# Neighbourhood attention on 4-row by 32-column key blocks, with values beside ones and the gated convolution run between the heads

## The chip, the cores and the metric

The kernel runs on the 8 cores of one Trainium2 chip, each core with its own part of the batch. The metric is the device time of the slowest core in microseconds (us). Most executions agree within 0.3%. Some fall in a slow state, in which the cores of one die get a lower clock; only fast executions are compared here (die 0 is cores 0 to 3, die 1 cores 4 to 7), and stage lengths are medians over the eight cores of the profiled execution.

Names: PE is TensorE (matmuls), ACT is ScalarE, DVE is VectorE, POOL is GpSimd, SP is SyncE, whose queue issues part of the DMAs; "POOLq" and "SPq" are the queues' issues. L0 to L3 are the four layers; 0 and 2 are "even", 1 and 3 "odd". The even part of a layer is everything from its first projection to the end of its out-projection; its MLP follows. "Modulation tiles" are pieces of ada_w, the weights that give shift, scale and gate; a tile is 1024 x 512 weights.

## The reference, cut to what matters

```python
# four layers; two request groups share the weights: 512 prompt tokens and 1024 latent tokens
# (a grid of 16 rows x 64 columns) per core
for l in range(4):
    # c: one vector for the latent tokens, another for the prompts; ada_w[l]: 1024 x 6144
    sh1, sc1, g1, sh2, sc2, g2 = ada_mod(silu(c), ada_w[l], ada_b[l])
    h = rms_norm(y, norm1_g[l]) * (1 + sc1) + sh1
    if l % 2 == 0:
        bg, cg, xa, q, k, v = split(h @ w_in, 6)        # 512 columns each
        a = bg * short_conv(cg * xa, conv_w)            # the gated conv, width 3 over tokens
        q, k = rms_norm(q, gq), rms_norm(k, gk)         # per head, 8 heads of 64
        # prompt: dense attention.  latent: each query sees 8 rows x 16 columns of keys
        # around it (clamped at the edges), with a relative bias, plus 256 cached keys,
        # all in one softmax
        mix = concat([a, att]) @ w_out
    else: ...                                            # pooling and latent attention, not touched
    y = y + g1 * mix
    y = y + g2 * sq_relu_mlp(rms_norm(y, norm2_g[l]) * (1 + sc2) + sh2, w1[l], w2[l])
```

## The kernel before

A program builder records operations with what they read and write, and a list scheduler fixes, before the run, the order of each engine by a "key" (lower goes first among what is ready in its model). Every engine then runs its own list strictly in order. The parts that the change and the argument touch:

```python
NW = 2                                  # two weight buffers of 1024 x 512 bf16, used in turn
def wtile(srcs, key=None):
    s = wt_i[0] % NW; wt_i[0] += 1      # strict turn: tile n waits until tile n-2 is used up
    DMA("pool", [(WT[s][...], src) ...], [], [bWT[s]], "wt%d" % s)

def norm(l, which, tb, key=None):       # 512 tokens, 8 slices of 128 features
    # ... sum of squares, rstd ...
    for kc in range(8):
        STT(tm, yT[:, kc], A, rstd, mult, mult)              # DVE, fp32
        ACT(hT[:, kc], tm, AF.Identity, bias=shift)          # ACT, to bf16

def even_layer(l, extra_steps):         # extra_steps: layer 0's own eight ada_w tiles
    for j in range(4):                  # gated conv, all of it ahead of the attention
        w = wtile(...)                  # ... 9 groups of 8 matmuls, DVE and ACT work
    for which in (q, k):                # q, then k: project, square, sum by matmul, scale
        # ... and for k a second projection in token order, for the output
    for tt in range(12): ...            # values, token order
    for ex in extra_steps: ex()
    # attention, one latent head: 2 query halves x (6 key tiles of 2 rows x 64 columns + 2 cached)
    for tile in tiles:                  # scores of 512 queries
        MMG(scores); ACT(P, scores, Exp); TT(P, P, table, mult)      # table = exp(bias) x mask
    for tile in tiles:
        MMG(po, V_tile, P)              # values
        MMG(pd, ones, P)                # the softmax sum, as a matmul of its own
    out_proj(...)

def mlp(l, with_ada):
    # 16 weight tiles through wtile; the next layer's 12 ada_w tiles through two buffers
    # of their own in the arena (AW), one step after each half of the work
```

Of the kernel before, what the change touches and what calls it, by code (L numbers as in the profile page):

```python
# [18 lines left out]
class Buf:  # L19

    __slots__ = ("name", "lw", "rd", "excl", "tile")

    def __init__(self, name, excl=False, tile=None):
        self.name = name
        self.lw = []
        self.rd = []
        self.excl = excl
        self.tile = tile


class PV:
# [9 lines left out]
    def rearrange(self, s, **kw):  # L41
        return PV(self.tile, self.chain + ((1, s, kw),))
# [47 lines left out]
class Prog:  # L90
# [18 lines left out]

    def region(self, lo, hi, n=1, name="r"):  # L110

        prior, keep = set(), []
        for (a, b, bl) in self.regions:
            if a < hi and lo < b:
                for x in bl:
                    prior.update(x.lw)
                    prior.update(x.rd)
                if not (lo <= a and b <= hi):
                    keep.append((a, b, bl))
            else:  # L120
                keep.append((a, b, bl))
        out = self.bufs(n, name)
        for x in out:
            x.lw = sorted(prior)
        keep.append((lo, hi, out))
        self.regions = keep
        return out

    def add(self, engs, fns, reads, writes, dur, kind="op", key=None, sem=None, nbytes=0):
# [6 lines left out]
        deps = set()  # L136
        for b in reads:
# [180 lines left out]
    def emit(self):  # L318
# [10 lines left out]
        for nd in self.seq:  # L329
            e = nd.eng  # L330
            kn = know[e]
            need = {}
            for d in sorted(nd.deps, key=lambda d: -nodes[d].fin):
# [50 lines left out]
def _const_tables():  # L384
    kc = np.arange(64)[:, None]
    qc = np.arange(64)[None, :]
    qcs = np.clip(qc - 8, 0, 48)
    colvalid = ((kc >= qcs) & (kc < qcs + 16)).astype(np.float32)
    MF = np.zeros((128, 14, 64), np.float32)
    MI = np.zeros((128, 14, 64), np.float32)  # L390
    for a in range(2):
        for ei in range(14):
            e = 6 - ei
            if -7 <= e + a <= 7:
                MF[a * 64:(a + 1) * 64, ei, :] = colvalid
            if -4 <= e + a <= 3:
                MI[a * 64:(a + 1) * 64, ei, :] = colvalid
# [22 lines left out]
    return dict(MF=MF.reshape(128, 896), MI=MI.reshape(128, 896), PA=PA.reshape(128, 2560), CS=CS,  # L420
# [3 lines left out]
def _rpb_expand(rpb):  # L424
    a = np.arange(128)[:, None, None] // 64
    kc = np.arange(128)[:, None, None] % 64
    e = 6 - np.arange(14)[None, :, None]
    qc = np.arange(64)[None, None, :]
    dr = np.clip(e + a + 7, 0, 14) + 0 * qc
    dc = np.clip(kc - qc + 15, 0, 30) + 0 * e  # L430
    out = rpb[:, :, dr, dc]
    return np.ascontiguousarray(out.transpose(0, 2, 1, 3, 4)).reshape(2, 128, 8 * 896)


def build(depth=4):
# [26 lines left out]
    gktok = din("gktok", (128, 128))  # L462
    rpbx = din("rpbx", (2, 128, 8 * 896))
    MFd = din("MF", (128, 896))
    MId = din("MI", (128, 896))
# [24 lines left out]
    with ExitStack() as st:  # L490
# [24 lines left out]
        gktok_sb = sb("gktok_sb", (128, 2, 64))  # L515
# [12 lines left out]
        rstd = [sb("rstd%d" % i, (128, 512)) for i in range(2)]  # L528
# [137 lines left out]

        def DMA(q, pairs, reads, writes, sem, out=False, key=None):
# [23 lines left out]
        def wtile(srcs, key=None):  # L691
            s = wt_i[0] % NW
            wt_i[0] += 1
            DMA("pool", [(WT[s][:, 0:src.shape[1], c0:c0 + nc_], src) for (c0, nc_, src) in srcs], [], [bWT[s]],
# [8 lines left out]
        def rstd_from(ss, bss, npart, ncol, inv_n, key=None):  # L703
            i = rs_i[0] % len(rstd)
            rs_i[0] += 1
            r, br = rstd[i], brstd[i]
# [10 lines left out]
               (gktok_sb[:], gktok.rearrange("p (i d) -> p i d", i=2)),  # L717
# [63 lines left out]
        def norm(l, which, tb, key=None):  # L781
# [11 lines left out]
            for kc in range(8):  # L793
# [3 lines left out]
                ACT(hT[:, kc, blk(tb)], tm[:], AF.Identity, [btm, bmw], [bh[tb][kc]],  # L797
                    bias=mod[:, l, sh0 + kc, m:m + 1], key=key)
# [383 lines left out]
        def even_layer(l, extra_steps):  # L1182
# [11 lines left out]
            V, bV = ar.take((128, 14, 512), BF16, 14, "V")  # L1194
            sqr = Ring([ar.take((128, 512), BF16, 1, "sq") for _ in range(2)])
            MFs, bM = ar.take((128, 896), BF16, 1, "MF")
            MIs, bM2 = ar.take((128, 896), BF16, 1, "MI")
            ost = Ring([ar.take((128, 512), F32, 1, "ost")])
            u0 = ar.off
            cgb, bcg = ar.take((128, T), F32, 1, "cg")  # L1200
            ub, bub = ar.take((128, T), F32, 1, "ub")
# [3 lines left out]
            segs = [(0, 256), (256, 512), (512, 1536)]  # L1205
            for j in range(4):
                w, bw = wtile([(0, 128, W[:, :, j * 128:(j + 1) * 128]),
                               (128, 128, W[:, :, 512 + j * 128:512 + (j + 1) * 128]),
                               (256, 128, W[:, :, 1024 + j * 128:1024 + (j + 1) * 128])])
                pr = lambda tb, o: [(w[:, kc, o:o + 128], hT[:, kc, blk(tb)]) for kc in range(8)]  # L1210
                for tb in range(3):
                    pt = PT(P)
                    MMK(pt[:], pr(tb, 128), [bw] + bh[tb], [pt.b])
                    COPY(cgb[:, blk(tb)], pt[:], [pt.b], [bcg], eng="act")
                for tb in range(3):
                    pt = PT(P)
                    MMK(pt[:], pr(tb, 256), [bw] + bh[tb], [pt.b])
                    TT(ub[:, blk(tb)], pt[:], cgb[:, blk(tb)], ALU.mult, [pt.b, bcg], [bub])
                ACT(cgb[:], ub[:], AF.Identity, [bub, bsm], [bcg], scale=cw[:, i, 1, j:j + 1])
                for (s0, s1) in segs:  # L1220
                    STT(cgb[:, s0 + 1:s1], ub[:, s0:s1 - 1], cw[:, i, 0, j:j + 1], cgb[:, s0 + 1:s1],
                        ALU.mult, ALU.add, [bub, bcg, bsm], [bcg])
                    STT(cgb[:, s0:s1 - 1], ub[:, s0 + 1:s1], cw[:, i, 2, j:j + 1], cgb[:, s0:s1 - 1],
                        ALU.mult, ALU.add, [bub, bcg, bsm], [bcg])
                for tb in range(3):
                    pt = PT(P)
                    MMK(pt[:], pr(tb, 0), [bw] + bh[tb], [pt.b])
                    TT(aT[:, j, blk(tb)], pt[:], cgb[:, blk(tb)], ALU.mult, [pt.b, bcg], [baT[tb][j]])
            LOADC([(kcT[:], nakT[i].rearrange("p (c t) -> p c t", c=4))], [bkc], q="pool")
            LOADC([(V[:, 12:14, :], nav[i].rearrange("(c p) n -> p c n", p=128))], bV[12:14], q="pool")  # L1230
            LOADC([(MFs[:], MFd)], [bM], q="pool")
            LOADC([(MIs[:], MId)], [bM2], q="pool")
            P.key = K + 2
            qv = qTm.rearrange("p (j two) t -> p j two t", two=2)
            for tb_ in range(3):
                MEMSET(qv[64:128, :, 0, blk(tb_)], 0.0, bq[tb_])
                MEMSET(qv[0:64, :, 1, blk(tb_)], 0.0, bq[tb_])
            for which, gain in ((3, gqna_sb), (4, gkna_sb)):
                w, bw = wtile([(0, 512, W[:, :, which * 512:(which + 1) * 512])])
                for j in range(4):  # L1240
                    for tb in range(3):
                        pt = PT(P)
                        MMK(pt[:], [(w[:, kc, j * 128:(j + 1) * 128], hT[:, kc, blk(tb)]) for kc in range(8)], [bw] + bh[tb], [pt.b])
                        sq, bsq = sqr.next()
                        ACT(sq[:], pt[:], AF.Square, [pt.b], [bsq])
                        p2 = PT(P)
                        MMK(p2[:], [(bdiag[:], sq[:])], [bsq, bconst], [p2.b])
                        r, br = rstd_from(p2[:], p2.b, 128, 512, 1.0 / 64)
                        if which == 3:
                            for a in range(2):  # L1250
                                ps_ = slice(a * 64, a * 64 + 64)
                                STT(qTm[ps_, 2 * j + a, blk(tb)], pt[ps_, :], gain[ps_, i:i + 1], r[ps_, :], ALU.mult, ALU.mult,
                                    [pt.b, br, bsm], [bq[tb][2 * j + a]])
                        else:
                            STT(kT[:, j, blk(tb)], pt[:], gain[:, i:i + 1], r, ALU.mult, ALU.mult, [pt.b, br, bsm], [bk[tb][j]])
                if which == 4:
                    for tt in range(4):
                        pt = PT(P)
                        MMK(pt[:], [(hT[:, kc, tt * 128:(tt + 1) * 128], w[:, kc, :]) for kc in range(8)], [bw] + bh[0], [pt.b])
                        o, bo = ost.next()  # L1260
                        ACT(o[:], pt[:], AF.Square, [pt.b], [bo])
# [26 lines left out]
            for ex in extra_steps:  # L1288
                P.key = K + 31
                ex()  # L1290
# [173 lines left out]
```

## Time and profile before

| | before |
|---|---|
| median of fast runs | 2731.5 us (2730.2 to 2736.1) |
| even part of layer 0, of layer 2 | 348.5, 332.1 us |
| the four MLPs | 351.6, 352.7, 351.0, 335.8 us |
| the two odd parts | 283.1, 279.9 us |
| start, up to the first projection | 82.4 us |

A stage is read like this (stretches of the kernel before, the even parts of layers 0 and 2 on its slowest core; columns: start:end, length, then busy us and count of PE, PE weight loads, DVE, ACT, POOL, then the granted clock as a share of full speed, the DMA engines' share (packet times over the engines' time, so it can exceed 1), GB/s):

```profile
83.90:435.30 351.40, 304.27 (x1558) 138.28 (x1587) 182.29 (x387) 207.95 (x369) 33.38 (x41) 0.95 0.45 70
1425.50:1758.20 332.70, 288.59 (x1310) 127.84 (x1334) 178.03 (x378) 205.10 (x364) 38.65 (x41) 0.98 0.32 51
```

PE is busy for 87% of both. The layers run the same code, but layer 0 also loads and uses eight modulation tiles; it is 16 us longer, and its DMA share is 0.45 instead of 0.32.

### The profile page before, as it was taken

The page shows a single profiled execution, that of the slowest core. Times are in us where ns is not written, and L with a number is a line of the kernel's source. Part 1 is how long each engine was busy: PE and PEld are TensorE (multiplying, and loading weights), DVE is VectorE, ACT ScalarE, POOL GpSimd, SP SyncE. Part 2 cuts the span into 40 slices and gives each one's busy share as a digit, 9 for nine tenths or more (in the row PEclk, how much of TensorE's full clock was granted, in tenths as well). Part 3 has the DMA queues.
Part 4 walks back from the last instruction along what each step waited for, and adds up shares of the span by engine and source line. Part 5 has one row for each costly group of instructions (what it writes and reads, how often), then busy time and mean ns, then how long its engine had stood idle before and what let it go on. Part 6 is the DMA issues. An engine that isn't in the chain of part 4 may idle for free.

```text
span 2729.1 us, 39242 instructions; the slowest of 8 cores (2711.3 to 2729.1 us)
## 1 busy us (share of the span) xinstructions
PE 2425.8 (89%) x14026; PEld 1153.1 (42%) x14266; DVE 1222.4 (45%) x2028; ACT 1171.4 (43%) x1866; POOL 246.0 (9%) x315
## 2 busy tenths in 40 slices
PE   1689799999986788999998888999999869899999
PEld 0234334444443454444433333444444435444444
DVE  0553555444455315443454547544345623354443
ACT  2347765112266596122142688512214748632111
POOL 2100010000003100000011100100100120000000
PEclk9899999999999899999999999999999979999999
DMA  9434936346412206456543222554552120133334
GB/s 181 49 45 77 148 54 99 62 78 103 67 30 33 39 2 94 68 80 104 86 61 39 51 50 36 88 80 78 94 88 41 33 46 1 16 47 62 47 47 124
DMA packets 190413, 179.39 MB, mean 66 GB/s; under 512 B 42320, under 2 KB 178512, under 8 KB 190224
## 3 DMA queue, kind: packets, MB, share of 16 engines
q0 software_dynamic: 174032, 149.34, 37.0%
q1 hardware_dynamic: 16192, 27.53, 3.3%
q8 instruction: 119, 1.95, 0.3%
q14 instruction: 70, 0.57, 0.1%
HBM read 312.90 MB, written 11.67 MB: 119 GB/s over the span
## 4 chain that ended last, share of the span: by engine, by line
PE 75%; ACT 7%; DMA 7%; issue 4%; DVE 4%; SPq 2%; POOL 1%; DVEq 0%; ACTq 0%; POOLq 0%
PE psall L595 75%; ACT arena L619 5%; DMA WT<-even_w_in 2%; DMA WT<-ada_w 2%; SPq L668 2%; DMA WT<-mlp_w 1%; DVE arena L630 1%; ACT rstd L619 1%; DMA arena<-ada_w 1%; ACT hT L619 1%; DVE ntmp L641 1%; POOL rtmp L630 1%; PE psall L603 1%; DVE arena L641 0%; POOL arena L630 0%
## 5 line engine op out<-in xcount | busy, mean ns | idle before, releaser
L595 PE MATMUL psall<-hT,WT 128*128 128x512 bf16 x4734 | 1084.4, 384 | 37.9 <-ACT hT L619 22.7
L619 ACT ACTIVATE arena<-psall 128x512 bf16<-128x512 f32 (+4 forms) x919 | 535.3, 611 | 1132.7 <-PE psall L595 1050.6
L595 PEld LDWEIGHTS psall<-hT,WT 128*128 128x128 bf16 x4848 | 475.2, 99 | 609.3 <-issue 66.9
L595 PE MATMUL psall<-arena,WT 128*128 128x512 bf16 x3199 | 714.2, 380 | 7.1 <-DMA WT<-mlp_w 3.2
L641 DVE SCALAR_TENSOR_TENSOR yT<-psall,mod,yT 128x512 f32<-128x512 f32 x480 | 360.1, 751 | 464.3 <-PE psall L595 464.1
L595 PEld LDWEIGHTS psall<-arena,WT 128*128 128x128 bf16 x3264 | 318.4, 98 | 387.7 <-issue 7.2
L595 PE MATMUL psall<-arena 128*128 128x65 bf16 (+6 forms) x2914 | 394.6, 267 | 67.5 <-ACT arena L619 36.0
L641 DVE SCALAR_TENSOR_TENSOR arena<-psall,arena 128x512 bf16<-128x512 f32 x384 | 264.2, 691 | 385.1 <-ACT arena L619 385.1
L595 PEld LDWEIGHTS psall<-arena 128*128 128x128 bf16 (+1 forms) x2936 | 186.6, 98 | 226.0 <-issue 121.9
L619 ACT ACTIVATE arena<-psall,rk 128x1024 bf16<-128x1024 f32 (+1 forms) x224 | 189.4, 951 | 14.7 <-PE psall L595 14.1
L668 POOL DMA_DIRECT2D WT<-mlp_w x64 | 56.0, 875 | 1311.9 <-PE psall L595 1291.6
L619 ACT ACTIVATE nsq<-yT 128x1024 bf16<-128x1024 f32 x96 | 99.6, 1053 | 137.3 <-PE psall L595 107.8
L641 DVE SCALAR_TENSOR_TENSOR ntmp<-yT,A,rstd 128x512 f32<-128x512 f32 x192 | 135.8, 747 | 37.5 <-ACT rstd L619 20.5
L619 ACT ACTIVATE hT<-ntmp,mod 128x512 bf16<-128x512 f32 x192 | 131.4, 717 | 44.0 <-DVE ntmp L641 43.3
L630 DVE TENSOR_TENSOR arena<-arena 128x256 bf16<-128x256 bf16 (+1 forms) x352 | 116.2, 356 | 42.0 <-ACT arena L619 23.0
L595 PE MATMUL psall<-WT,hT 128*128 128x512 bf16 (+1 forms) x631 | 113.0, 331 | 22.5 <-ACT hT L619 7.8
L595 PE MATMUL psall<-arena,ones 128*128 128x512 bf16 (+1 forms) x348 | 118.5, 370 | 10.1 <-ACT arena L619 4.6
L619 ACT ACTIVATE rstd<-rstd 128x512 f32<-128x512 f32 (+2 forms) x148 | 85.7, 580 | 7.1 <-ACT rstd L619 0.7
L595 PEld LDWEIGHTS psall<-WT,hT 128*128 128x128 bf16 x640 | 50.7, 101 | 81.3 <-issue 32.9
L603 PE MATMUL psall<-ident,arena 128*128 128x128 bf16 (+1 forms) x316 | 29.2, 245 | 51.9 <-POOL arena L630 44.8
L595 PE MATMUL psall<-sTb,WT 128*128 128x2 bf16 x384 | 11.6, 164 | 66.0 <-DVE gqr_sb L635 49.8
L619 ACT ACTIVATE rstd<-psall,eps_sb 128x512 f32<-128x512 f32 x84 | 57.4, 683 | 28.4 <-PE psall L595 27.8
(86 smaller groups left out, 912.7 us busy)
## 6 DMA issues: line engine op xcount, KB each, us to landing
WT<-mlp_w POOLq DMA_DIRECT2D x64, 1024.0 KB, 8.3
arena<-ada_w POOLq DMA_DIRECT2D x36, 1024.0 KB, 12.6
WT<-ada_w POOLq DMA_DIRECT2D x12, 1024.0 KB, 12.4
arena<-rpbx SPq DMA_DIRECT2D x16, 448.0 KB, 3.7
yT<-xT SPq DMA_DIRECT2D x3, 2048.0 KB, 25.6
WT<-even_w_in POOLq DMA_DIRECT2D x24, 256.0 KB, 5.9
WT<-even_w_in POOLq DMA_DIRECT2D x6, 1024.0 KB, 9.1
yT_out<-yT SPq DMA_DIRECT2D x6, 1024.0 KB, 4.1
```

Of the source, the lines that this page charges most:

```text
L595: h.matmul(R(out), lhsT=lhsT, rhs=rhs, start=start, stop=stop, skip_group_check=skip))
L603: fns = [lambda h, o=o, a=a: h.transpose(R(o), a, ident[:, :]) for (o, a) in items]
L619: return lambda h: h.activation(out=R(out), in_=R(in_), func=func, **kw)
L630: P.add(eng, [lambda h: h.tensor_tensor(out=R(out), in0=R(in0), in1=R(in1), op=op)], reads, writes, vdur(fsize(out), eng, isb(out, in0, in ...
L641: P.add("dve", [lambda h: h.scalar_tensor_tensor(out=R(out), in0=R(in0), scalar=scalar, in1=R(in1), op0=op0, op1=op1)], reads, writes, vdu ...
L668: fns = [lambda h, o=o, i_=i_: h.dma_start(out=o, in_=i_) for (o, i_) in pairs]
```

## The change

The intent is to take PE work off the even layers. Keys are stored in blocks of 4 rows x 32 columns; for each block the only queries that can see it are 40 columns wide, so scores and values are computed on strips of 8 or 12 rows x 40 columns. Values stand beside 64 columns of ones, so that one matmul gives the output and the softmax sum. The conv, which needs PE much and ACT little, is placed between the heads, which are the other way round. Queries and values are now projected first, keys after them; a second projection of the prompts' keys, only for the output, is gone. Some of the norms' shift-adds (and multiplications of the conv) may run on POOL, and a POOL instruction now waits for the one before it.

```diff
+        def SHIFT(out, in_, v, op, reads, writes, key=None):
+            P.add(("act", "dve", "pool"), {"act": [fa], "dve": [fv], "pool": [fv]}, reads, writes,
+                  {"act": act_dur(out, v, None), "dve": ..., "pool": vdur(n, "pool") + 0.1}, key=key)   # model: 0.685 us
@@ norm
-                ACT(hT[:, kc, blk(tb)], tm[:], AF.Identity, [btm, bmw], [bh[tb][kc]], ...)
+                SHIFT(hT[:, kc, blk(tb)], tm[:], mod[...], ALU.add, [btm, bmw], [bh[tb][kc]], key=key)
@@ even_layer
-            V, bV = ar.take((128, 14, 512), BF16, 14, "V")
+            Vx, bv_ = ar.take((128, 14, 4, 192), BF16, 29, "V")     # value | ones | value per head pair
+            MEMSET(Vx[:, :, :, 64:128], 1.0, [bones])
+            def v_tile(vt):
+                # ... prompt tiles straight; latent tiles by way of a buffer (two in turn):
+                v_, bv = vtr.next()
+                EVAC(v_[:], pt[:], [pt.b], [bv])
+                # 2 column blocks x 2 rows x 2 heads = 8 small DMAs put 32 tokens each in their block
+                DMA("sp", prs, [bv], [...], "vx%d" % (vt % 4))
+            conv_zone = [6, 7]                     # two PSUM banks kept for the conv
+            P.key = K + 15                         # after the heads' keys (K + 10 to K + 12): a filler
+            for j in range(4):
+                w, bw = wtile(...)                 # the conv's tile
+                # ...
+                for ex in extra_steps[2 * j:2 * j + 2]:
+                    ex()                           # layer 0: two modulation tiles after each
+            RG = [(0, 8, 0, 4), (0, 12, 0, 0), (4, 16, 1, 0), (8, 16, 1, 0)]     # query rows per key block
+                        MMG([(scores strip of 40 columns) for b in range(2)], ...)
+                        ACT(pv, sv, AF.Exp); TT(pv, pv, tv, ALU.mult)
+                        # values and sum in one: stationary = vo(...) = 64 values beside 64 ones
 # cuts marked by "..." and by comments
```

## The prediction

> **What bounds the kernel now.** I read the page first (busy shares, the 40 slices, the chain that ended last), then the groups by shape, then the chain in order of time inside the two even layers, then a table of stretches.
>
> ```profile
> PE 2425.8 (89%) x14026; PEld 1153.1 (42%) x14266; DVE 1222.4 (45%) x2028; ACT 1171.4 (43%) x1866; POOL 246.0 (9%) x315
> PE   1689799999986788999998888999999869899999
> ACT  2347765112266596122142688512214748632111
> DMA  9434936346412206456543222554552120133334
> PE 75%; ACT 7%; DMA 7%; issue 4%; DVE 4%; SPq 2%; POOL 1%; DVEq 0%; ACTq 0%; POOLq 0%
> ```
>
> TensorE (PE) is busy in nearly every slice, and three quarters of the chain are its matmuls. So what a change takes off PE counts almost in full, so long as nothing else becomes the wait there. One slice is 68 us: the first even layer is slices 1 to 5, the second 20 to 25.
>
> The price of a matmul comes from the chain inside the even layers:
>
> ```profile
> 223.03 10.74 PE psall L595 x49
> 233.82 10.74 PE psall L595 x49
> 1556.52 10.74 PE psall L595 x49
> ```
>
> 49 matmuls of 512 columns in 10.74 us are 0.219 us each. (The group's mean of 384 ns is latency, as matmuls are pipelined.) I price PE by columns: 0.219 us per 512.
>
> Where the even layers idle shows in the stretches (start:end, length, then busy us and count of PE, PEld, DVE, ACT, POOL, then clock, DMA share, GB/s):
>
> ```profile
> 200.00:256.00 56.00, 53.06 (x239) 24.26 (x245) 19.32 (x27) 35.64 (x66) 6.14 (x6) 0.97 0.30 60
> 256.00:300.00 44.00, 31.13 (x320) 17.80 (x322) 19.93 (x57) 32.60 (x72) 4.71 (x6) 0.91 0.95 146
> 300.00:340.00 40.00, 34.63 (x209) 15.77 (x211) 26.59 (x82) 30.62 (x58) 2.62 (x3) 0.93 0.81 139
> 1487.00:1550.00 63.00, 52.83 (x237) 22.95 (x241) 34.47 (x48) 35.05 (x60) 5.17 (x5) 1.00 0.35 59
> 1590.00:1640.00 50.00, 37.83 (x192) 16.76 (x193) 29.06 (x84) 44.62 (x93) 0.70 (x1) 1.00 0.21 40
> 1640.00:1706.00 66.00, 55.52 (x243) 23.75 (x246) 45.90 (x144) 56.05 (x108) 3.48 (x4) 1.00 0.22 37
> ```
>
> The attention (256 to 383 and 1590 to 1706) keeps ScalarE (ACT) up to 89% busy, and PE waits there for exponentials. In layer 0 the DMA engines are at 0.95 as well: eight modulation weight tiles (ada_w) go through the two weight buffers. So the even layers are PE-bound, with ACT and, in layer 0, DMA close behind.
>
> **What the Trainium skill says.** "TensorE: Matmul & The Clock Gate", section "Wait — 56ns, not 53.3ns?": a warm matmul takes N / 2.4 GHz plus about 2.5 ns, 215.7 ns at 512 columns. The trace agrees (219). So strips of 160 to 480 columns should cost by their columns.
> "ScalarE: Activation LUTs", section "What ACT_TABLE_LOAD costs": an ACTIVATE takes 186 ns + 0.833 ns per column, and back-to-back ones overlap by about 93 ns. The trace agrees: 599 ns for 512 columns, 1053 for 1024, and seven of 512 in a row in 3.54 us, 0.51 each. Fewer, wider exponentials are cheaper.
> "VectorE: DVE Perf Modes", section "Mode 2×_1P — pack two bf16 into one 32-bit read": packed bf16 operands give two results per cycle. The mask multiplies fit it (256 columns in 283 ns, against 684 for 512 from PSUM).
> "DMA: Bandwidth & Descriptors", section "Specifications": transfers under 512 B fall below line rate and turn into read-modify-write. No run here isolates it yet; the new copies of V are made of 128 B pieces.
>
> **The change part by part**, for one even layer (there are two).
>
> 1. **Attention on PE.** Before, a latent head does 2 query halves x 8 key tiles x 3 matmuls (scores, values, ones) x 512 columns = 24,576 columns. After, scores take 3,200 columns (strips of 8, 12, 12, 8 rows x 40 columns x 2 column blocks), values 3,200, the context keys 2 x 2,048: 10,496. The ones come free, as the stationary tile now holds values beside ones. Eight heads save 112,640 columns. The prompt heads go from 3,072 to 2,048 each: 8,192 saved. The second key projection (token order, only for the output) goes: 32 matmuls, 16,384 columns. Sum 137,216 columns = 268 x 0.219 = 58.7 us. The order of instructions of both kernels confirms the sum over two layers (704 matmuls gone, 320 strips new). **Two layers: 117.5 us of PE work.**
>
> 2. **ACT in attention.** By 0.07 us + 0.833 ns per column (the pitch fitted to 0.50 at 512): a latent head has two exponentials of 1,024, two of 960, two of 640, four tables of 480, and Ln and Exp of 1,024 for the denominator: about 8.5 us, 68 for eight heads, against 77 + 20 + 8 = 105 before (128 x 0.60, 16 x 1.2, 8 x 0.95). Per head PE has 10,496 columns = 4.5 us. Alone the heads would thus be ACT-bound; this is why the gated convolution (36 groups of 8 matmuls, 63 us) is run between them.
>
> 3. **The convolution as filler.** In layer 2 the order puts about 9 groups beside the key projection, 11 beside the prompt heads and the rest, then 8 out-projection groups, into the first six latent heads. Heads: PE 36 + 28 + 14 = 78 us against ACT 68 + 6; about 86 us with latencies. The last two heads have no filler: about 8 us lost.
>
> 4. **Weights.** The key weights reuse the query's buffer and are loaded only after the last query matmul. Such a load took 9.1 us; nearly nothing covers it: 6 to 9 us idle per layer. Before, three such loads stood in the chain but cost PE only 1.5 + 2.0 + 2.1 us.
>
> 5. **Copies of V.** 64 small DMAs per layer, 8 for each of 8 latent V tiles, 128 pieces of 128 B each. Old small DMAs took 0.33 to 0.59 us to issue; at 0.4, a tile needs 3.2 us on the queue, against 3.7 us of PE work between V tiles (17 matmuls). By packets: hardware packets cost 3.3% x 16 x 2729 / 16,192 = 89 ns; 1,024 x 89 / 16 = 5.7 us per tile. It may just keep up, or hold the evacuations back; I put 5 us per layer.
>
> 6. **DVE and POOL.** Mask work falls from 160 x 0.28 + 32 x 0.27 + 16 x 1.09 = 71 us to about 16 x 0.48 + 16 x 0.65 = 18 per layer; DVE was not the bound. 52 of 192 shift-adds of the norms move to POOL, where a 512-column cast took 0.61 us: no worse than ACT's 0.72. No gain, perhaps 4 us of loss.
>
> **Sum.** Second even layer now: 1425 to 1706, 281 us, holding 1064 + 64 matmul equivalents (247 us) and 2 of norm: 32 idle. After: 58.7 less work; idle 4 (start) + 7 (keys) + 5 (V) + 12 (heads) + 6 (end) = 34. First: 84 to 383, 299 us: 247 + 10 (ada and norm) and 42 idle; after, 45, since about 30 MB (eight ada tiles and a weight tile of 2 MB, three conv tiles of 1.5, tables of 7.8) must come in some 100 us, and two ada tiles in flight took 12.6 us, 320 MB/ms. Net 117.5 - 2 - 3 - 4 = 108 us: 2731 - 108 = **2623 us**.
>
> **Rivals.**
> (a) **ACT takes over the heads**: a single accumulator and in-order exponentials make each head take ACT's 8.5 us plus 3 to 4 us of waits for the denominator. For it: the 89% of the stretch 1590 to 1640. Against: the filler has its own two banks. 8 heads x 2 layers x 2 us = 32 us back: 2655.
> (b) **V copies and table loads hold the queue**: tiles at 6 us instead of 3.7 make 18 us per layer, and a late table blocks ACT in order; tables are 32 per layer instead of 8. For it: the 89 ns per packet. Against: tables landed in 3.7 us. 2640 to 2670.
> (c) **Layer 0 becomes DMA-bound** at 0.95 share: 20 to 30 us of its gain lost, 2650.
> (d) **Better than summed**: queries and values of the first token block come first, so the norm of the other blocks is hidden (before, PE waited 9.1 us there): 2605.
>
> **Range and chances.** PE's 117 us is near certain. (a) to (c) could each take 20 to 35 and are partly exclusive; (d) gives 10 to 20. I take 2623, 2580 to 2672. Faster by over 2% means below 2677: 0.88; within 2%: 0.10; slower: 0.02.
>
> **What will show it.** PE matmul columns down by 137,216 per layer, and strips priced by columns; spans of both even layers about 56 us shorter, MLP and odd layers equal; heads with PE over 80% busy; one idle of 6 to 9 us for the key weights; V tiles at 4 us with little wait for arena copies. Wrong if: strips run slower than by columns, evacuations wait for the copies by over 10 us per layer, ACT over 95% with PE under 75% in the heads, or norms lengthened by POOL elsewhere.

## The result

| | before | after |
|---|---|---|
| median of fast runs | 2731.5 us | 2673.0 us (2668.9 to 2675.0) |
| ratio of fast runs | | 0.978 (95%: 0.976 to 0.980) |
| even part of layer 0 | 348.5 | 334.4 |
| even part of layer 2 | 332.1 | 280.3 |
| the four MLPs | 351.6, 352.7, 351.0, 335.8 | 352.6, 354.5, 354.2, 342.4 |
| the two odd parts | 283.1, 279.9 | 279.2, 283.2 |
| start | 82.4 | 76.5 |

A ratio is the mean time of one kernel's fast runs over that of the other's in the same rounds, so it isn't quite the ratio of the medians; stage lengths are from the profiled run. The kernel is faster by 2.2%. The predicted 2623 was 50 us too low, and the result lies 1 us beyond the upper end of the range.

The page of the kernel after (busy shares, the 40 slices, and the chain that ended last by engine):

```profile
PE 2343.6 (88%) x13818; PEld 1117.1 (42%) x13818; DVE 1125.4 (42%) x1644; ACT 1079.8 (40%) x1586; POOL 375.1 (14%) x407
PE   1777768999987788999997798999998779899999
ACT  2566514111266595121145576411126659522111
DMA  9356794346312205556533546555631220233334
PE 72%; DMA 6%; ACT 6%; issue 4%; POOL 4%; DVE 4%; SPq 3%; DVEq 0%; POOLq 0%; ACTq 0%
```

PE is busy for 82 us less than before, but slices 1 to 5, the even part of layer 0, show only sevens and a six, and slice 5 has DMA at 9. POOL is now 4% of the chain and was 1%.

The stretches of the kernel after (columns as above): the even parts of layers 0 and 2, and one pause inside layer 0.

```profile
78.00:418.80 340.80, 254.06 (x1489) 120.15 (x1488) 139.45 (x204) 171.72 (x244) 61.67 (x74) 0.88 0.61 99
1405.20:1686.50 281.30, 237.43 (x1108) 108.88 (x1109) 130.03 (x186) 172.02 (x246) 62.16 (x67) 0.93 0.48 82
333.00:361.00 28.00, 2.46 (x75) 2.13 (x74) 1.02 (x2) 0.00 (x0) 5.93 (x10) 0.56 1.20 158
```

Both layers lost about 50 us of PE busy time. In layer 2 that is the gain, 52 us. In layer 0 only 14 us of it came out, and between 333 and 361 us PE stands almost still while the DMA engines are full. The clock column has fallen too, from 0.98 to 0.93 in layer 2.

What holds PE in that pause (the chain in order of time: start, us, what):

```profile
283.45 12.75 DMA WT<-even_w_in
...
333.80 26.84 DMA WT<-ada_w
```

The second line is the last of layer 0's own modulation tiles. In PE's fixed order it stands behind the first two modulation steps of the *next* layer, and all their loads are in flight at once.

The second surprise is POOL. The groups by shape: output<-input, count, busy us and mean ns of one, idle time before it and what ended it; then the chain at the norm that follows layer 3's odd part:

```profile
L622 ACT ACTIVATE hT<-ntmp,mod 128x512 bf16<-128x512 f32 x132 | 92.0, 721 | 81.7 <-DVE ntmp L644 81.6
L672 POOL TENSOR_SCALAR hT<-ntmp,mod 128x512 bf16<-128x512 f32 x52 | 100.1, 1924 | 131.7 <-DVE ntmp L644 123.9 <-POOL hT L672 6.0 <-DVE mod L633 1.0
```

```profile
2326.76 2.07 POOL hT L672
...
2329.04 2.07 POOL hT L672
...
2331.32 2.07 POOL hT L672
```

The same shift-add takes 0.72 us on ACT and 1.92 us on POOL. Five of them stand one after another there, 2.28 us apart (three are shown); PE runs out of other work during the third and waits 4.9 us for hT.

The third is the issue of the value copies (SP's queue: count, then minimum, median and maximum ns of one issue):

```profile
L679 SPq DMA_DIRECT2D arena<-arena x142: 562/601/1886, 90.6 to 2158.1; - x142
L679 SPq DMA_DIRECT2D arena<-rpbx x64: 327/328/952, 185.8 to 1630.1; - x64
```

A plain table load takes 0.33 us to issue, a copy from SBUF to SBUF 0.60. Eight of them with their gaps make 5.1 us per value tile, while PE needs 3.7 us for the work between two tiles.

So there were four suspects: the order of layer 0's loads, POOL, the value copies, and whatever lowers the clock.

### The profile page after: what moved, and what is told of

The parts are those of the page before. It is cut to its first block, busy times and chain, and to the rows that moved or that the text cites. A ratio compares the mean times of both kernels' runs of the same rounds, so it can differ in the third digit from the quotient of the medians.

```text
span 2670.9 us, 37465 instructions; the slowest of 8 cores (2654.4 to 2670.9 us)
## 1 busy us (share of the span) xinstructions
PE 2343.6 (88%) x13818; PEld 1117.1 (42%) x13818; DVE 1125.4 (42%) x1644; ACT 1079.8 (40%) x1586; POOL 375.1 (14%) x407
## 4 chain that ended last, share of the span: by engine, by line
PE 72%; DMA 6%; ACT 6%; issue 4%; POOL 4%; DVE 4%; SPq 3%; DVEq 0%; POOLq 0%; ACTq 0%
PE psall L598 72%; ACT arena L622 4%; SPq L679 3%; POOL hT L672 2%; DMA WT<-ada_w 2%; DMA WT<-even_w_in 1%; DMA WT<-mlp_w 1%; DVE arena L633 1%; DVE ntmp L644 1%; ACT rstd L622 1%; PE psall L606 1%; POOL rtmp L633 1%; ACT hT L622 0%; DVE arena L644 0%; POOL arena L633 0%
## 5 line engine op out<-in xcount | busy, mean ns | idle before, releaser
L598 PE MATMUL psall<-hT,WT 128*128 128x512 bf16 x4656 | 1065.5, 387 | 58.1 <-POOL hT L672 23.0
L622 ACT ACTIVATE arena<-psall 128x512 f32<-128x512 f32 (+6 forms) x721 | 470.8, 662 | 1114.0 <-PE psall L598 1055.2
L598 PE MATMUL psall<-arena,WT 128*128 128x512 bf16 x3456 | 759.5, 381 | 3.6 <-DMA WT<-mlp_w 2.0
L598 PEld LDWEIGHTS psall<-hT,WT 128*128 128x128 bf16 x4656 | 458.3, 99 | 618.3 <-issue 108.9
L598 PEld LDWEIGHTS psall<-arena,WT 128*128 128x128 bf16 x3456 | 337.8, 98 | 412.5 <-issue 12.5
L598 PE MATMUL psall<-arena 128*128 128x65 bf16 (+9 forms) x2872 | 324.9, 261 | 53.9 <-ACT arena L622 23.8
L622 ACT ACTIVATE hT<-ntmp,mod 128x512 bf16<-128x512 f32 x132 | 92.0, 721 | 81.7 <-DVE ntmp L644 81.6
L672 POOL TENSOR_SCALAR hT<-ntmp,mod 128x512 bf16<-128x512 f32 x52 | 100.1, 1924 | 131.7 <-DVE ntmp L644 123.9
L598 PE MATMUL psall<-WT,hT 128*128 128x512 bf16 (+1 forms) x576 | 99.8, 329 | 12.2 <-ACT hT L622 7.2
L598 PE MATMUL psall<-nsq,ones 128*128 128x512 bf16 x192 | 57.8, 418 | 16.5 <-ACT nsq L622 16.5
## 6 DMA issues: line engine op xcount, KB each, us to landing
WT<-ada_w POOLq DMA_DIRECT2D x12, 1024.0 KB, 13.3
```

Of the source, the lines that this page charges most:

```text
L598: h.matmul(R(out), lhsT=lhsT, rhs=rhs, start=start, stop=stop, skip_group_check=skip))
L622: return lambda h: h.activation(out=R(out), in_=R(in_), func=func, **kw)
L672: fv = lambda h: h.tensor_scalar(out=out, in0=in_, scalar1=v, scalar2=None, op0=op)
```

## The experiments

Each was run beside the kernel before on the same chip; the kernel before had 2732.9 to 2734.4 us there, so totals of two runs can differ by some 3 us for the chip alone. Totals are medians of fast runs (e4, e5, e6, e9, e10, e11 and e12 had one slow execution each, left out); stage lengths are from the profiled run.

| run | total | even L0 | even L2 | four MLPs | ratio to before |
|---|---|---|---|---|---|
| kernel after | 2673.0 | 334.4 | 280.3 | 352.6, 354.5, 354.2, 342.4 | 0.978 |
| e1, no shift-add on POOL | 2640.7 | 328.0 | 277.5 | 347.4, 348.1, 348.1, 336.0 | 0.967 |
| e2, next layer's loads held | 2654.0 | 315.6 | 281.3 | 355.1, 354.6, 354.5, 342.2 | 0.972 |
| e4, seven of layer 0's loads left out | 2635.5, disturbed | 290.2 | 280.6 | 354.3, 355.0, 354.8, 342.6 | 0.967 |
| e5, values without copies | 2679.3, disturbed | 323.1 | 272.7 | 366.8, 354.4, 355.1, 342.3 | 0.981 |
| e6, conv ahead of the heads | 2676.7 | 315.2 | 300.4 | 355.4, 355.5, 354.4, 341.9 | 0.979 |
| e7, three mends | 2627.5 | 316.1 | 270.2 | 348.3, 348.3, 348.2, 336.3 | 0.961 |
| e8, PE kept busy in one pause | 2671.7 | 332.5 | 279.9 | 352.5, 354.8, 353.6, 342.3 | 0.977 |
| e9, e7 and two tiles later | 2609.7 | 302.8 | 271.2 | 349.5, 348.7, 348.0, 336.7 | 0.955 |
| e12, ada tiles first, nothing else | 2647.6 | 304.4 | 281.7 | 357.3, 355.8, 354.2, 342.1 | 0.969 |
| e10, e9 with L0's conv ahead | 2620.9 | 317.9 | 268.4 | 348.9, 348.8, 348.0, 335.9 | 0.959 |
| e11, e9 with ada tiles first | 2596.8 | 286.5 | 270.1 | 349.7, 349.0, 348.0, 336.4 | 0.950 |

### e1: no shift-add on POOL

```diff
-            P.add(("act", "dve", "pool"), {"act": [fa], "dve": [fv], "pool": [fv]}, ...
+            P.add(("act", "dve"), {"act": [fa], "dve": [fv]}, ...
```

> Edit: the shift-adds of the norms and of the gated conv may go to ACT or DVE only, never to POOL. Theory P (a POOL shift-add takes 1.92 us against about 0.7 on ACT, and runs of five to twelve of them stand in the chain at the ends of the norms): the PE pauses behind hT from POOL, 4 to 6 us at four norm ends and some smaller ones, go; total 12 to 25 us less, about 2655, with the MLP stages 2 to 5 us shorter each. Rival (POOL was a real relief): ACT gets 52 x 0.7 = 37 us more work and the time stays within 5 us or grows.

Measured: 2640.7 us, 32 less than the kernel after. Every MLP stage, which holds the ends of the norms, is 5.2 to 6.4 us shorter; layer 0 is 6.4 and layer 2 is 2.8 us shorter. The groups of e1 show who took the 52 over:

```profile
L622 ACT ACTIVATE hT<-ntmp,mod 128x512 bf16<-128x512 f32 x174 | 119.5, 717 | 36.3 <-DVE ntmp L644 35.9 <-issue 0.2
L672 DVE TENSOR_SCALAR hT<-ntmp,mod 128x512 bf16<-128x512 f32 x18 | 8.6, 484 | 0.9
```

ACT took 42 of them and DVE 10, at 0.72 and 0.48 us each, and ACT's idle time before them fell from 81.7 to 36.3 us. The theory held, and its size was too small: the gain exceeds the 12 to 25 us expected. The scheduler had POOL at 0.685 us in its model and handed it work it took 1.92 us for. In the trace the duration does not follow what DVE does at the same time: an instruction with 19% of its time beside a busy DVE took 1.76 us and one with 84% took 1.55 us, so sharing with DVE does not explain it. Why this instruction is slow on POOL stays open. (The edit also takes four of the conv's multiplications off POOL, 2.0 and 3.0 us each; they are part of the 32 us.)

### e2: the next layer's loads held back

```diff
-                        DMA("pool", [(w[:], src)], [], [bw], s)
+                        DMA("pool", [(w[:], src)], [bmodB[l - 1]], [bw], s)   # after the layer's own modulation
```

> Edit: the loads of the next layer's modulation weights wait until the previous layer's modulation is finished, so in layer 0 they no longer go ahead of the last own modulation tile and the out-projection. Theory L1 (order of loads): the 26 us that PE stands between 333 and 361 us shrink to 10 or less, and the even part of layer 0 goes from 334 to about 318; all other stages unchanged; total about 2657. Rival L2 (the two weight buffers and the DMA engines' rate limit the layer, whatever the order): less than 6 us, and the pause only moves.

Measured: 2654.0, 19 less; the even part of layer 0 went from 334.4 to 315.6, against the 318 expected, and its MLP is 2.5 us longer, since the loads come later. The order of loads is a cause. It isn't all of it: 315.6 is still 34 us more than layer 2 of the same run.

### e4: layer 0's own modulation loads left out (wrong result)

```diff
+                    if slots is None and nt > 4:
+                        w, bw = hT[:, :, 0:512], bh[0][0]      # no load: any data already there
-                    if slots is None:
+                    elif slots is None:
```

> Wrong result on purpose. Edit: seven of the eight modulation tiles of layer 0 in the even part are computed from activations already in SBUF, so their 15 MB are never loaded; the matmuls stay. Theory L (the loads through two weight buffers took layer 0's gain): the even part of layer 0 falls from 334 to 280 to 292 us, the length that the same code has in layer 2 (280); total 2620 to 2630. Rival (layer 0 is long for another reason, as its cold start or the shift-adds): it stays above 310.

Measured: with seven of the eight loads left out, the even part of layer 0 is 290.2 us, inside the range expected, and 44 us less than with them. So that is what these seven loads, and the work that waits behind them, cost the kernel after. The total must not be read: in two of the four runs a pair of cores (4 and 5, then 2 and 3) was 31 to 64 us slower than the same cores in the profiled run, at a lower clock. The profiled run, in which no pair was hit, took 2631.1, 1 us above the expected range.

### e5: values written straight to their place (wrong result)

```diff
-                v_, bv = vtr.next()
-                EVAC(v_[:], pt[:], [pt.b], [bv])
-                # ... 8 small DMAs
+                EVAC(vpair(vt), pt[:].rearrange("p (j s e) -> p j s e", j=4, s=2), [pt.b], bV[vt])   # token order
```

> Wrong result on purpose. Edit: the latent value tiles are written from PSUM straight to their place, in token order, so the 64 small copies per even layer go away. Theory V (a copy takes 0.60 us to issue, eight of them 5.1 us per tile against 3.7 us of PE work, so the queue paces the value tiles): the query and value phase of both even layers shortens by 5 to 10 us each, and the half-rate matmuls that follow its pauses go too; total 10 to 20 us less. Rival (PE waits there for the norm and for weights anyway): under 4 us in total.

Measured: layer 0 is 11.3 us and layer 2 7.6 us shorter, 19 together: the upper end of what was expected. The total of 2679.3 says the opposite. The mean clock and span of the two dies in the profiled run:

```profile
die 0 (median of its cores): 2668.3 us, clock 0.943
die 1 (median of its cores): 2644.2 us, clock 0.956
```

On die 0 one stage alone, the MLP of layer 0, took 380 us on all four cores and 353 on die 1. The trace says why: for some 155 us of it the granted clock of these four cores is 0.81, and a matmul of 512 columns comes every 260 ns instead of every 216. In the other fast runs the spans of one pair of cores, or of three, are longer at a lower clock. On the undisturbed die the kernel takes 2634 to 2651 us, against 2654 to 2671 on the eight cores of the kernel after. The mechanism is shown by the stages; the total is left out. (Values in a wrong order passed the comparison with the reference. Its tolerance doesn't see them; this kernel is wrong all the same.)

### e6: the conv ahead of the heads again

```diff
-            conv_zone = [6, 7]
-            P.key = K + 15
+            conv_zone = None
+            P.key = K + 5
```

> Edit: one part of the change undone. The gated conv gets back its place ahead of the heads and all PSUM banks; the new key blocks, values beside ones and shift-adds stay. Theory F (alone, a latent head is paced by ACT at 8.5 us plus a wait for its denominator, against 4.5 us of PE work, so the conv between the heads is worth what PE would idle): heads at 9 to 11 us each, and the even part of layer 2 goes from 280 to 310 to 325 us; layer 0 by less, 10 to 30, as its loads are the limit; total 2715 to 2740, so most of the whole gain is lost. Rival (the removed PE columns are the gain, and the conv's place is worth little): less than 10 us per layer.

Measured: 2676.7 (2673.6 to 2682.5), no clear difference from the kernel after. Neither theory had it: layer 2 is 20 us *longer*, less than expected, and layer 0 is 19 us *shorter*. The stretches of e6, even parts of layers 0 and 2:

```profile
77.00:401.00 324.00, 257.11 (x1338) 118.60 (x1360) 133.57 (x196) 179.18 (x256) 50.42 (x66) 0.89 0.59 95
1394.50:1696.80 302.30, 246.90 (x1087) 111.32 (x1109) 129.08 (x184) 175.32 (x250) 55.97 (x65) 0.90 0.44 77
```

The ends of the heads tell why. In layer 2 the eight latent heads end 10.7 us apart with the conv ahead and 11.9 us apart with the conv between them. So a head alone takes 10.7 us, not much more than ACT's work for it (61.9 us in the time of seven heads on the slowest core, 8.8 each, where the prediction had 8.5), and 1.2 us more with its share of the conv and of the out-projection; the filler is worth 20 us in layer 2, where it is fed. In layer 0 the last head of the kernel after ends at 251 us of the stage, but the stage goes on to 334, 83 us; in layer 2 that tail is 34 us. With the conv ahead the tail of layer 0 is 34 us as well. So the 49 us more of tail seem to be work that had been waiting for loads while the heads ran. This is a new theory, which e12 tests: between the heads, a conv tile keeps its weight buffer as long as the heads take (four tiles over some seven heads of 11.9 us, so an estimate of 20 us), and the modulation tiles queue behind it. (A third weight buffer would test that directly. It needs 8 KB per partition and was not run; no run shows whether it fits.)

### e8: PE kept busy in one pause

```diff
+            if l == 2:
+                pw_ = PT(P)        # 36 matmuls that nothing reads, in the pause
+                MMG([(pw_[:], hT[:, kc % 8, 0:128], hT[:, kc % 8, blk(0)], kc == 0, kc == 35) for kc in range(36)],
+                    bh[0] + [bq[2][5]], [pw_.b], key=K + 1.95)
```

> Edit: in layer 2 only, 36 matmuls that nothing reads stand where PE pauses for the key weights (1465.7 to 1474.3 us, two pauses of 4.8 and 3.6 us, after which 12 matmuls came at 427 ns instead of 216). Theory W (after a pause PE runs at half rate for some microseconds, so a pause costs more than its length): the key projections then start at 216 ns each, and the even part of layer 2 gets 2 to 3 us shorter though PE does 7.8 us more work; number of slow matmuls in that stage down by about 12. Rival (the slow matmuls come from elsewhere, as shared power or SBUF traffic of the incoming weights): they stay at 427 ns, and the stage is as long or longer.

The stretches of the kernel after, then of e8, both on core 6: the pause or what fills it, and the 10.8 us that follow in two halves.

```profile
1465.70:1474.30 8.60, 0.77 (x2) 0.13 (x2) 1.73 (x3) 2.40 (x4) 2.58 (x3) 0.73 1.40 154
1474.30:1479.70 5.40, 5.40 (x13) 1.92 (x14) 0.01 (x1) 0.60 (x1) 0.00 (x0) 0.50 1.03 152
1479.70:1485.10 5.40, 5.40 (x26) 2.44 (x25) 1.67 (x3) 1.32 (x2) 0.00 (x0) 0.98 0.00 0
```

```profile
1453.10:1460.90 7.80, 7.77 (x37) 3.55 (x38) 0.00 (x0) 1.08 (x2) 0.53 (x1) 1.00 1.61 190
1460.90:1466.30 5.40, 5.40 (x27) 2.45 (x26) 1.50 (x2) 2.51 (x4) 0.00 (x0) 1.00 0.71 105
1466.30:1471.70 5.40, 5.40 (x27) 2.46 (x26) 2.62 (x5) 2.92 (x5) 0.00 (x0) 1.00 0.00 0
```

After the pause, 13 matmuls run in 5.40 us at a granted clock of 0.50, and then 26 in the same time. With the pause filled, it is 27 from the first. In the 55 us around that place the kernel after has 9 to 24 slow matmuls on each of the eight cores, e8 has none on six and 7 and 9 on two. So a pause costs PE its length and then about 2.8 us more (13 x 0.21). This is as "TensorE: Matmul & The Clock Gate" of the Trainium skill has it in "What's actually happening": after an idle window of about 3.4 us PE runs at half clock until it has been busy for such a window. The trace agrees: a matmul of 512 columns comes every 427 and then every 216 ns, and the clock record of this core has 0.50 for 10.2 us around the pause, three such windows, of which the last 5.4 us fall on matmuls.

The total did not show it: 2671.7 against 2673.0, and the stage is 0.4 us shorter where 2 to 3 were expected; that is within the scatter. Two things take the 2.8 us back: the filling outlasts the pause (from the issue of the loads to PE's next own matmul it is 11.0 us instead of 10.1, medians of the cores), and seven of the eight cores got 7 to 9 new slow matmuls some 210 us into the stage. What half-rate running explains is the clock column: the clock records of both kernels hold only 0.50 and 1.00. Summed over the 512-column matmuls that took over 420 ns instead of 379, the mean core lost 42 us to half-rate running before the change and 63 us after: 7 us more in layer 0 and 9 more in layer 2.

### e7: three mends at once

No shift-add on POOL (e1), the next layer's loads held (e2), and four buffers instead of two for values on their way to be copied:

```diff
-            vtr = Ring([ar.take((128, 512), BF16, 1, "vt") for _ in range(2)])
+            vtr = Ring([ar.take((128, 512), BF16, 1, "vt") for _ in range(4)])
```

> Three mends at once, correct result: no shift-add on POOL, the next layer's modulation loads held back, and four buffers instead of two for value tiles on their way to be copied. Theory: the first two measured 32 and 19 us alone; the copies go on pacing the queue but the evacuations no longer wait, 5 to 10 of the 19 us that the kernel without copies gained on undisturbed cores; the sum is 56 to 61: about 2615 (2605 to 2625). Rival (they share one wait, so the gains do not add): 2630 to 2640.

Measured: 2627.5 with a correct result, so between theory and rival. In layer 2 the gains add: 10.1 us is close to e1's 2.8 plus e5's 7.6, so two more buffers give all that leaving the copies out gave. In layer 0 they don't: 316.1 is e2's length and no better. There all of them had shortened waits for the same loads.

### e9: two tiles moved to the MLP

The gate of layer 0's MLP is not needed before the MLP's second half. Its two modulation tiles go through the MLP's own buffers (AW).

```diff
-                    which = "A" if nt < 4 else "B"
+                    which = "A" if nt < 4 else ("B" if nt < 10 else "C")    # C: tiles 10 and 11, in the MLP of layer 0
```

> The three mends of the run before, and the last two modulation tiles of layer 0 (gate of the MLP, 4 MB) moved from its even part into its MLP, where the loads have room. Theory L (bytes through the two buffers, 41 MB in some 165 us, limit the even part of layer 0): 6 to 12 us less than the three mends alone, all in that stage, total about 2605. Rival (after the hold, the loads are no longer the limit): within 3 us of the three mends.

Measured: 2609.7, 18 less than e7; layer 0 lost 13.3 us. Fewer loads help, more than expected. Whether it is their bytes or their place in the line, this run doesn't tell.

### e12, e10 and e11: the order of the tiles

e12 is the kernel after with nothing but this: in layer 0 the modulation tiles come before the conv's and all use the buffer that the value weights leave, beside the key projection.

```diff
+            if extra_steps:
+                P.key = K + 2.5
+                for ex in extra_steps: ex()          # through weight buffer 1 only
+                extra_steps = []; wt_i[0] += 1
             conv_zone = [6, 7]
```

> The changed kernel with one edit: in layer 0 the eight modulation tiles come ahead of the conv's weights and all through the one weight buffer that the value weights leave free, beside the key projection; the conv's tiles then follow as in layer 2. The same bytes and the same work. Theory H (as a filler between the heads, a conv tile holds its weight buffer some 20 us, and the modulation tiles wait in line behind it, so that after the last head some 49 us more of loads remain than in layer 2): the even part of layer 0 goes from 334 to 285 to 300 us, total 2625 to 2640. Theory B (the bytes are the limit, whatever the order): within 8 us of 334.

Measured: 304.4 us in layer 0, 30 less with the same bytes and the same matmuls (a little above the 285 to 300 expected), and 2647.6 in all, above the 2625 to 2640 expected; the MLP after it is 5 us longer. The even parts of layers 0 and 2 of e12:

```profile
78.00:383.60 305.60, 250.73 (x1358) 115.52 (x1357) 133.73 (x196) 174.32 (x250) 51.08 (x66) 0.90 0.61 100
1377.20:1660.40 283.20, 241.27 (x1108) 109.78 (x1109) 129.86 (x186) 172.38 (x246) 62.11 (x67) 0.92 0.48 82
```

The theory that the bytes are the limit falls: the order in which tiles pass the two buffers cost layer 0 30 us of its gain. It isn't all of the loss: the tail after the last head fell from 83 to 54 us, not to the 34 of layer 2.

e10 is e9 with the edit of e6 in layer 0 alone:

> The best kernel so far (2610), with the conv of layer 0 alone put ahead of the heads. Theory H: nothing paced by the heads holds a weight buffer any more, so the loads end before the heads do; the even part of layer 0, 303 us in the best kernel and 315 with the conv ahead alone, becomes 290 to 298; layer 2 stays at 271; total 2598 to 2606. Theory B: no change, within 3 us.

Measured: 2620.9; layer 0 has 317.9 us, 15 *more* than e9, where 5 to 13 less were expected. This is a miss for both theories. The first latent head ends at 193 us of the stage (160 in e9). My reading, which no run tests: now all the loads stand in front of the heads, with nothing that needs no weights to run beside them, and e6 was better not for having no filler, but for having its loads done by the time the heads came. Why two tiles fewer than in e6 changed nothing there stays open.

e11 is e9 with the order of e12:

> The best kernel so far (2610), with the modulation tiles of layer 0 ahead of the conv's, through one buffer beside the key projection, and the conv as a filler in both layers. Theory H: the even part of layer 0 goes from 303 to 275 to 288 us, close to the 271 of layer 2; total 2582 to 2596. Theory B: within 3 us of 2610.

Measured: 2596.8 us, correct, 5.0% faster than before and 2.9% faster than the kernel after; layer 0 at 286.5 us, inside the 275 to 288 expected, the total 0.8 us above its range. Even parts of layers 0 and 2, and the chain of e11 by engine:

```profile
78.10:369.10 291.00, 242.47 (x1297) 114.30 (x1296) 137.48 (x204) 173.57 (x249) 38.93 (x59) 0.92 0.61 98
1348.20:1621.70 273.50, 233.33 (x1108) 107.73 (x1109) 132.30 (x190) 174.94 (x249) 45.53 (x60) 0.94 0.49 85
```

```profile
PE 77%; ACT 6%; DMA 6%; issue 4%; DVE 3%; SPq 2%; POOL 2%; DVEq 0%; ACTq 0%; POOLq 0%
```

The DMA share of layer 0 is the 0.61 of the kernel after, in 50 us less: on the average the engines were not the limit. PE is 77% of the chain and was 72%.

## Why the prediction was right and where it was wrong

- **"Attention on PE": right.** Busy time fell by 50 us in layer 0 and 51 in layer 2, where 58.7 each were predicted. Most of the rest is half-rate running, which counts as busy: with the 7 and 9 us more of it (e8) the work taken off is some 57 and 60 us, an estimate from the two. The pitch of a warm 512-column matmul is still 216 ns, and a strip of 480 columns has 203, so strips are priced by their columns. Layer 2 gave 52 of the 56 us predicted.
- **"ACT in attention" and "The convolution as filler": right mechanism, a bit small.** A head alone takes 10.7 us (e6), of which ACT works 8.8 for it; rival (a) had 8.5 and 3 to 4 of waits. With the filler eight heads take 95 us instead of the 86 predicted. The filler is worth 20 us in layer 2 (e6).
- **"Weights": the size right, the wait another, a term left out.** Layer 2 has a pause of 8.6 us, at the upper end of 6 to 9, but it isn't the key weights that end it. The conv's first tile is loaded ahead of them, and PE goes on with the conv; the key weights land some 5.4 us after that tile and are covered. On six of the eight cores the conv's weights had landed 1.0 to 2.4 us before PE went on: there ACT, held up by the value copies, ended the pause. Without the copies (e5) PE goes on 0.25 us after that landing, and the pause is 5.8 to 7.0 us. What the prediction had no line for is the half-rate running after it: 2.8 us for each such pause (e8), 20 us more in all than before.
- **"Copies of V": mis-sized by its issue price.** 0.4 us was assumed and 0.60 measured, so 5.1 us per tile instead of 3.2; the 5 us put per layer were 11 and 8 (e5). The scheduler's own model has 0.07 us for such an issue, so it could not see the queue. The row cited there from "DMA: Bandwidth & Descriptors" pointed at the wrong term: the copies landed 1.9 us after issue, and the issues queued. (The same page has, in "Why small descriptors are slow (HBM only)", that copies within SBUF do not suffer from small pieces.) The other half of rival (b), late tables, came too: in layer 0 ACT waited 13.8 us for tables while the heads ran, in layer 2 2.4.
- **"DVE and POOL": the largest wrong price.** "No worse than ACT's 0.72" was inferred from a POOL cast of the same shape, 0.61 us. The shift-add took 1.92, and in all 32 us where "perhaps 4" had been allowed (e1). The last risk on the prediction's own list, norms lengthened by POOL elsewhere, is what happened: the MLP stages were to be equal and grew by 1 to 7 us.
- **"First: 45 idle", the term for layer 0: the step that failed.** 56 us of gain were summed (58.7 of work, less 3 of idle time) and 14 came. The prediction compared bytes with time, found room, and gave rival (c) 20 to 30 us. The loss was there and larger, but not by the route named: the DMA engines were not the bound. Tiles that the heads pace held the two buffers, and the next layer's loads went ahead: 30 us from order alone with the same bytes (e12), 19 from holding back the next layer (e2), all of these with fewer tiles, POOL and the copies mended 48 of 334 (e11).
- **Rival (d)**: the start is 6 us shorter. Whether by its mechanism, no run tests.
- **The 50 us, by stage:** layer 0 fell short of its sum by 42 us and layer 2 by 5; the MLPs grew by 13, of which 4 had been allowed; the start gave back 6. Only the start worked the other way, and layer 0 is most of the miss.

The terms do not add up: 32 (POOL, e1), 19 (loads held, e2) and 19 (copies, e5) are 70 us measured one by one, while these three mends in e7 together gave 45. They add in layer 2; in layer 0 they seem to shorten waits for the same loads. What the kernel still loses in layer 0 (286.5 against 270.1 in layer 2, of which the modulation matmuls themselves are a part) was not taken apart further.

## What to carry to other kernels

Price an operation that moves to another engine by that very instruction on that engine; a cast of the same shape was off by a factor of three. When work is made a filler, ask what it holds while it waits: here it held one of two weight buffers, and everything behind it in the line. A pause of PE of more than a few microseconds costs its length and the slow matmuls after it, so a change that takes work off PE and opens pauses gives some of it back.

## What the Trainium skill lacked or had wrong

- "GPSIMD Engine Reference", section "4.1 Engine selection", has elementwise work with one input as "roughly line-rate" on GpSimd. A cast of 128x512 from fp32 to bf16 agrees (0.61 us); a tensor-scalar add with a per-partition operand in the same shape took 1.92 us (1.55 to 2.06), against 0.72 on ACT and 0.48 on DVE.
- No page that I found gives the issue time of a DMA from SP by its form ("DMA: Bandwidth & Descriptors" has one figure for every copy, in a section on a later chip): 0.33 us for a table load of 240 KB, 0.60 us for an SBUF to SBUF copy of 32 partitions in pieces of 128 B. Here the issue was the limit and not the transfer.
- "TensorE: Matmul & The Clock Gate", section "Seeing it yourself", has a limiter that takes a whole die to 13/16 of the clock, and says to expect that clock for sustained dense matmuls on all cores, on the default power profile. The state is there: in e5 the four cores of die 0 ran some 155 us of one MLP at 0.81. But it isn't the rule here: in the profiled runs of both kernels all eight cores go through the MLPs (336 to 355 us each) at 0.99 to 1.00.
- No page that I found has a state of two cores: in e4 and e5 the spans of one pair of neighbouring cores are 20 to 64 us longer than in the profiled run, at a lower mean clock, in runs that mostly count as fast. These runs have no trace, so what lowers that clock isn't shown.
